# Compressed keys streamed in front of the selected keys, the root's table moved, and the last half block cut in two

## The chip, the cores and the metric

The kernel runs on one core of a Trainium2 chip. The metric is the device time of one execution, in microseconds; lower is better. The kernel before took 977.5 us in the median of three runs (976.83 to 977.7).

The core has a matrix engine (PE, with PEld for its weight loads), a vector engine (DVE), an activation engine (ACT), a general engine (POOL) and a queue engine (SP). Each follows its own fixed list of instructions in order, and semaphores make them wait for one another.

## The reference

One transformer block, in fp32, over 512 tokens of width 1024: a gated feed-forward layer, a mixer with two kinds of attention, a second gated feed-forward layer, and a last normalization.

```python
x = x + 0.5 * swiglu(rmsnorm(x, norm_ffn1), w_gate1, w_up1, w_down1)
x = x + hybrid_mixer(rmsnorm(x, norm_mix), w_in, ..., w_out, rel_bias)
x = x + 0.5 * swiglu(rmsnorm(x, norm_ffn2), w_gate2, w_up2, w_down2)
return rmsnorm(x, norm_final)
```

The mixer has 8 heads of block attention ("MoBA") and 8 heads that add up three attentions over the same query ("NSA"). For an NSA head:

```python
k_cmp = silu(blocks(kc_raw) @ w1_k) @ w2_k               # 31 compressed keys of each group
lg_cmp = q @ k_cmp.T * scale + bias(d_cmp)               # 512 x 31, masked
o_cmp = softmax(lg_cmp) @ v_cmp
o_slc = softmax(q @ ks.T * scale + bias, causal) @ vs    # selected keys: with 512 tokens, all of them
o_win = softmax(q @ kw.T * scale + bias, causal) @ vw    # window keys
out = g0 * o_cmp + g1 * o_slc + g2 * o_win
```

Four heads share one group of keys; there are two groups.

## The kernel before

Every fp32 matrix product is made of products of rounded parts: a value is split into a rounded high part and the remainder (`halves`, ACT line 92 and DVE line 96, or POOL line 94 while `side[0]` is set), and three products (`mm3`, lines 101 to 103) are added in PSUM. For logits, queries and keys are stacked instead: a tile of 128 partitions holds a 64-row part on the one half and its partner on the other (`stack_q`, `stack_k`). `stack_k` copies a half to the other 64 partitions by DMA (line 660).

The program has three stages: the first feed-forward layer, the mixer (it starts near 345 us and ends near 640 us), the second feed-forward layer. PE's list in the mixer is woven from two streams. One is `work`, a stream of projections (`pp`, `pv`, `pc`), the compression of keys and values, and the output projections (`pw`); it runs by the quotas of `target`. The other is `steps`: for each NSA head three chunks with the selected keys (kind "ks"), three with the window keys ("kw"), and after the odd head's "ks" chunks a step for the compressed keys of the pair of heads (`cmp_pair`); then three chunks for each MoBA head. A chunk is one of the groups of query blocks `QIS = ((0, 1), (2,), (3,))`. Each step has three parts: `logits`, `turn` four steps later and `values` seven steps later. The final order of instructions on each engine is set by the framework's own timeline model, so an edit in one place can shift the order in the whole mixer.

A chunk's `logits` takes one of the two PSUM banks of tag "s", multiplies a query block with the keys up to its diagonal (lines 948 and 949, the two stacked key tiles; 128, 256, 384 or 512 columns), then adds the bias and takes the row minimum in one DVE instruction from PSUM (line 954), exponentiates on ACT (956), inverts the sum on DVE (958) and scales on POOL (963). `turn` transposes on PE (972), `values` multiplies with the values (115, 116).

For the compressed keys, `second` (line 805 on) splits the 64 x 64 result `pck` into the tile `kc` with one ACT and one DVE instruction (814, 815) and one DMA (816). `cmp_pair` multiplies, for each of four query blocks and two heads, the query block with 64 columns of `kc` into a bank "s" of its own (line 1011), adds bias and remainder in two DVE instructions of 256 elements (1015, 1016) into the tile `c`, and goes on with a softmax over 32 columns, the transposes (1032) and the values.

The window keys, the selected keys, the token-major values and later the MoBA outputs share twelve tiles `kvn`.

At the end, the last feed-forward product of each of four token blocks `i` comes in two halves of 512 columns (`pd`, six matmuls each). `residual` adds it on DVE (1162) and squares it on ACT with a row sum (1163); after half 1, `norm` takes the root on ACT (1167), inverts it on DVE (1168), scales half 0 on ACT (1170) and half 1 on DVE (1171), and two DMAs on the queue of SP write the block out (1173). The first root needs another ACT table than silu did, which is loaded just ahead of it.

Of the kernel before, what the change touches and what calls it, by code (L numbers as in the profile page):

```python
# [15 lines left out]
S = 512  # L16
# [13 lines left out]
def block_kernel(ctx: ExitStack, tc: tile.TileContext, A: dict, out: bass.AP):  # L30
# [576 lines left out]
    with ExitStack() as ph:  # L607
# [58 lines left out]
        def kvn():  # L666
            return kv.tile([128, S], F32R, name="kvn", tag="kvn", bufs=12)

        def nsa_k(key):
            def then(p):  # L670
                got[key] = stack_k(scaled(p, None), [kvn() for _ in range(4)])
            return then
# [73 lines left out]
        def compress(which):  # L746
# [58 lines left out]
            def second(w):  # L805
                hh, hl = p[2]
                pp = pt(tag, "pck")
                if which == 0:
                    for c in range(2):
                        with held():  # L810
                            mm3(pp[:64, :64], w[c], (hh[:, c], hl[:, c]), c == 0, c == 1)
                    yield
                    a = kv.tile([128, 2, 64], F32R, name="kc")
                    nc.scalar.activation(a[0:64, 0], pp[:64, :64], AF.Copy)
                    nc.vector.tensor_tensor(a[0:64, 1], pp[:64, :64], f32(a[0:64, 0]), ALU.subtract)
                    nc.sync.dma_start(f32(a[64:128]), f32(a[0:64]))
                    got["kc"] = a
                    return
# [93 lines left out]
        def halves_turned(width):  # L912
# [3 lines left out]
                    for name in ("th", "tl")]  # L916

        def chunks_of_head(h, kind, first, last):

# [6 lines left out]
            def logits(qis):  # L926
# [10 lines left out]
                else:  # L937
                    lp = ap.tile([128, 384], F32, name="lpn", tag="lpn", bufs=4)
                at_, wide = {}, 0
                for qi in qis:  # L940
                    at_[qi] = slice(wide, wide + (qi + 1) * 128)
                    wide += (qi + 1) * 128
                for qi in qis:
                    n = (qi + 1) * 128
                    w = at_[qi]
                    lps[qi] = lp[:, w]
                    q = aq[:, qi * 128:(qi + 1) * 128]
                    nc.tensor.matmul(s[:, w], q, ak[at][:, :n], start=True, stop=False)
                    latest[0] = nc.tensor.matmul(s[:, w], q, ak[2 + at][:, :n], start=False, stop=True)
                for qi in qis:  # L950
                    n = (qi + 1) * 128
                    w = at_[qi]
                    m = ap.tile([128, 4], F32, name="m", tag="m", bufs=8)
                    nc.vector.tensor_tensor_reduce(lp[:, w], s[:, w], tb[:, S - n:], -1.0, 3.0e38,
                                                   ALU.add, ALU.min, m[:, 0:1])
                    nc.scalar.activation(lp[:, w], lp[:, w], AF.Exp, bias=m[:, 0:1], scale=-1.0,
                                         accum_out=m[:, 1:2])
                    nc.vector.reciprocal(m[:, 2:3], m[:, 1:2])
# [40 lines left out]
        def cmp_pair(pair):  # L999
# [4 lines left out]
            def logits():  # L1004
                need("kc")
                s = pt("s", "ps_c")
                sv = s.rearrange("p (i h e n) -> p i h e n", i=NT, h=2, e=2)
                for i in range(NT):
                    for odd in range(2):
                        q = got["n", pair][odd][:, i * 128:(i + 1) * 128]  # L1010
                        nc.tensor.matmul(sv[:, i, odd], q, got["kc"][:, :, g * 32:(g + 1) * 32],
                                         start=True, stop=True)
                c = st["c"] = ap.tile([128, NT, 2, 32], F32, name="c", tag="c", bufs=1)
                m = ap.tile([128, 3, NT, 2], F32, name="mc", tag="mc", bufs=2)
                nc.vector.tensor_tensor(c, sv[:, :, :, 0], cb[:, :, 2 * pair:2 * pair + 2, :], ALU.add)
                nc.vector.tensor_tensor(c, c, sv[:, :, :, 1], ALU.add)
                nc.vector.tensor_reduce(m[:, 0], c, AX.X, ALU.max)
# [105 lines left out]
    with ExitStack() as ph:  # L1123
# [35 lines left out]

        def residual(i, half, p):  # L1160

            nc.vector.scalar_tensor_tensor(z[i, half], p, 0.5, z[i, half], ALU.mult, ALU.add)
            nc.scalar.activation(sq, z[i, half], AF.Square, accum_out=ss[:, half, i:i + 1])  # L1163

        def norm(i):
# [6 lines left out]
            for half in range(2):  # L1172
                nc.sync.dma_start(out[i * 128:(i + 1) * 128, half * S:(half + 1) * S], y[half])

# [5 lines left out]
        for i in range(NT):  # L1180
            b = slice(i * 128, (i + 1) * 128)
            for half in range(2):
                p = pt(None, "pd")
                for k, f in enumerate(last):
                    mm3(p, (hs[f][0][:, b], hs[f][1][:, b]), w[half][k], f == last[0], f == last[-1])
                residual(i, half, p)
                if half == 0:
# [91 lines left out]
```

## Time and profile before

| | us |
|---|---|
| median of three runs | 977.5 |
| the profiled execution | 977.13 |
| its span, first to last instruction | 975.3 |
| mean granted TensorE clock | 0.998 |

The profile is of one execution. A row of the timeline starts with its start in us from the span's start, its length, the engine, the line, the operation, and "output<-inputs"; rows of the same kind that follow one another are merged with a count. Matmuls overlap, so the distance from one start to the next, not the length, is what a matmul takes.

| stretch of the mixer, us | DVE busy | ACT busy | POOL busy |
|---|---|---|---|
| 360 to 390 | 22.4 | 18.0 | 0.2 |
| 540 to 570 | 19.3 | 26.3 | 27.5 |
| 600 to 640 | 32.2 | 25.7 | 9.5 |

There are eleven table loads on ACT in the span, each about 1.28 us.

### The profile page before, as it was taken

What the parts mean: (1) busy time and instruction counts of PE and PEld (TensorE: products, weight loads), DVE (VectorE), ACT (ScalarE), POOL (GpSimd) and SP (SyncE); (2) the same over time, 40 slices, a digit from 0 to 9 for tenths busy, and PEclk for the clock granted to TensorE, in tenths of its full rate; (3) what the DMA queues carried; (4) which work ended last, traced back from release to release, by engine and by line L of the source; (5) the groups of instructions that cost most, each with busy time, mean ns of one, the idle gap of its engine ahead of it and who ended that gap; (6) DMA issues with size and microseconds to landing.
All of it is one profiled execution on the core that took longest, in us unless ns stands there. A gap on an engine that the chain in (4) does not pass through costs nothing.

```text
span 975.3 us, 18446 instructions
## 1 busy us (share of the span) xinstructions
PE 962.4 (99%) x6852; PEld 891.4 (91%) x6852; DVE 761.3 (78%) x1557; ACT 565.0 (58%) x1171; POOL 158.6 (16%) x202
## 2 busy tenths in 40 slices
PE   9999999999999999999999999999999999999996
PEld 7789999999999999889888888888999999999995
DVE  6897997788787488867778677889799778778753
ACT  6464664454554366677776886656466445554435
POOL 0000000000000000056777897100000000000002
PEclk9999999999999999999999999999999999999999
DMA  7255544332411225641312332235354423241102
GB/s 259 89 198 160 210 134 136 95 107 80 124 60 53 59 74 148 193 143 40 92 28 71 88 97 71 65 109 194 88 169 134 131 65 106 90 130 44 55 12 87
DMA packets 51599, 104.62 MB, mean 107 GB/s; under 512 B 10129, under 2 KB 16738, under 8 KB 51508
## 3 DMA queue, kind: packets, MB, share of 16 engines
q1 hardware_dynamic: 51220, 102.91, 33.7%
q8 instruction: 54, 0.88, 0.4%
q10 hardware_dynamic: 288, 0.52, 0.2%
q14 instruction: 37, 0.30, 0.1%
HBM read 97.98 MB, written 5.30 MB: 106 GB/s over the span
## 4 chain that ended last, share of the span: by engine, by line
PE 92%; DVE 4%; DMA 2%; ACT 1%; issue 1%; POOL 0%; SPq 0%; ACTq 0%; DVEq 0%; POOLq 0%
PE pd L110 16%; PE pu L101 7%; PE pu L103 7%; PE pu L102 7%; PE pw L103 5%; PE pw L101 5%; PE pw L102 5%; PE pgu L101 3%; PE pgu L102 3%; PE pgu L103 3%; PE pd L102 3%; PE pd L103 3%; PE pd L101 3%; PE ps_t L972 3%; PE pv L103 2%; PE pv L101 2%
## 5 line engine op out<-in xcount | busy, mean ns | idle before, releaser
L242 ACT ACTIVATE sph<-aw 128x512 fp32r<-128x512 f32 x252 | 157.3, 630 | 190.4 <-issue 58.6
L243 DVE TENSOR_TENSOR spl<-aw,sph 128x512 fp32r<-128x512 f32 x252 | 171.2, 686 | 60.2 <-ACT sph L242 57.0
L92 ACT ACTIVATE whi<-raw 128x512 fp32r<-128x512 f32 (+2 forms) x202 | 122.2, 615 | 111.0 <-PE pd L110 33.5
L110 PE MATMUL pd<-h,whi 128*128 128x256 f32 x896 | 138.1, 276 | 0.0
L96 DVE TENSOR_TENSOR wlo<-raw,whi 128x512 fp32r<-128x512 f32 (+1 forms) x166 | 109.1, 666 | 19.8 <-ACT whi L92 16.1
L101 PE MATMUL pu<-th,sph 128*128 128x256 f32 x432 | 119.6, 277 | 0.3 <-ACT wc L352 0.3
L103 PE MATMUL pu<-th,spl 128*128 128x256 f32 x432 | 119.4, 276 | 0.0
L102 PE MATMUL pu<-tl,sph 128*128 128x256 f32 x432 | 119.4, 276 | 0.0
L110 PEld LDWEIGHTS pd<-h,whi 128*128 128x128 f32 x896 | 118.3, 188 | 0.1
L328 DVE TENSOR_TENSOR aw<-aw 128x512 f32<-128x512 f32 x144 | 98.0, 682 | 0.0
L110 PE MATMUL pd<-h,wlo 128*128 128x256 f32 x448 | 87.2, 276 | 0.0
L540 DVE SCALAR_TENSOR_TENSOR x<-pd,x 128x512 f32<-128x512 f32 x88 | 59.9, 684 | 29.6 <-PE pd L110 22.2
L101 PEld LDWEIGHTS pu<-th,sph 128*128 128x128 f32 x432 | 81.1, 188 | 1.2 <-ACT wc L352 0.5
L102 PEld LDWEIGHTS pu<-tl,sph 128*128 128x128 f32 x432 | 81.1, 188 | 0.6
L103 PEld LDWEIGHTS pu<-th,spl 128*128 128x128 f32 x432 | 81.1, 188 | 0.1
L101 PE MATMUL pw<-xo,sph 128*128 128x256 f32 x288 | 79.6, 277 | 0.6 <-ACT sph L242 0.6
L102 PE MATMUL pw<-xo,sph 128*128 128x256 f32 x288 | 79.5, 277 | 0.0
L103 PE MATMUL pw<-xo,spl 128*128 128x256 f32 x288 | 79.4, 277 | 0.0
L110 PEld LDWEIGHTS pd<-h,wlo 128*128 128x128 f32 x448 | 67.4, 188 | 0.0
L881 POOL MEMSET tb<- 128x256 f32 x16 | 4.9, 308 | 332.1 <-DVE x L540 329.0
L1188 POOL TENSOR_SCALAR mean<-ss 128x1 f32<-128x1 f32 x4 | 1.2, 296 | 350.2 <-ACT sqd L1163 350.2
L101 PEld LDWEIGHTS pw<-xo,sph 128*128 128x128 f32 x288 | 54.1, 188 | 1.9 <-ACT sph L242 0.8
(249 smaller groups left out, 2675.8 us busy)
## 6 DMA issues: line engine op xcount, KB each, us to landing
aw<-in_wg SPq DMA_DIRECT2D x72, 256.0 KB, 3.6
aw<-in_wu SPq DMA_DIRECT2D x72, 256.0 KB, 4.7
raw<-in_wd1a SPq DMA_DIRECT2D x20, 512.0 KB, 4.4
raw<-in_wd2a SPq DMA_DIRECT2D x20, 512.0 KB, 5.0
raw<-in_w_a SPq DMA_DIRECT2D x16, 512.0 KB, 3.6
raw<-in_w SPq DMA_DIRECT2D x8, 512.0 KB, 3.6
raw<-in_w_o SPq DMA_DIRECT2D x8, 512.0 KB, 4.0
raw<-in_wg SPq DMA_DIRECT2D x7, 512.0 KB, 3.6
```

The source lines that it names most:

```text
L92: last_hi[0] = nc.scalar.activation(hi, v, AF.Copy)
L96: nc.vector.tensor_tensor(lo, v, f32(hi), ALU.subtract)
L101: nc.tensor.matmul(p, w[0], v[0], start=first, stop=False, skip_group_check=again)
L102: nc.tensor.matmul(p, w[0], v[1], start=False, stop=False, skip_group_check=again)
L103: return nc.tensor.matmul(p, w[1], v[0], start=False, stop=last, skip_group_check=again)
L110: nc.tensor.matmul(p[:, h], a, b[:, h], start=first and n + i == 0, stop=last and n == 2, skip_group_check=True)
L242: nc.scalar.activation(hi, v, AF.Copy)
L243: self.last_lo = nc.vector.tensor_tensor(lo, v, f32(hi), ALU.subtract)
L328: nc.vector.tensor_tensor(to, x, y, op)
L540: nc.vector.scalar_tensor_tensor(xs[d], p, 0.5, xs[d], ALU.mult, ALU.add)
L881: nc.gpsimd.memset(t[:, :S - 256], 0.0)
L972: latest[0] = nc.tensor.transpose(p[:, wide:wide + 128], lps[qi][:, j * 128:(j + 1) * 128], ident)
```

## The change

**Mixer.** Four tiles `kst` of 64 + 512 columns hold the stacked selected keys of the two groups in columns 64 to 575, and the compressed keys of the group in front of them: the high part in columns 32 to 63, its remainder in columns 0 to 31. The write of the compressed keys is done group by group: two ACT instructions in place of one, four of DVE in place of one, four DMAs in place of one. A "ks" chunk's product for query blocks 0, 1 and 2 starts 32 columns earlier, so that its first 32 columns are the compressed logits; for block 3, whose 512 columns fill a bank, one extra product of 64 columns is put into the free rest of block 2's bank. The compressed logits are read from there into `acc`, a tile that is otherwise only used for the sums of squares, by four small DVE instructions for each head (lines 990, 992, 993 and 994 of the new kernel). The own products, the own bank and the two DVE instructions of `cmp_pair` go; its softmax goes on in `acc`, one half for even pairs and one for odd. "ks" chunks now need the compressed keys to be there. `kvn` has eight tiles in place of twelve.

**End.** A root of one column is issued behind the last silu, so that the root's table is loaded there. The very last half block (block 3, half 1) is computed as two parts of 256 columns, each with its own bank, residual and square; the first part's sum is added to `mean` by one more ACT instruction. The first of the last block's two output DMAs is issued by ACT's queue.

```diff
         def kvn():
-            return kv.tile([128, S], F32R, name="kvn", tag="kvn", bufs=12)
+            return kv.tile([128, S], F32R, name="kvn", tag="kvn", bufs=8)
+        CK = 32
+        keys = slice(2 * CK, 2 * CK + S)
+        kst = [kv.tile([128, 2 * CK + S], F32R, name="kst", tag="kst", bufs=4) for _ in range(4)]
...
-                    a = kv.tile([128, 2, 64], F32R, name="kc")
-                    nc.scalar.activation(a[0:64, 0], pp[:64, :64], AF.Copy)
-                    nc.vector.tensor_tensor(a[0:64, 1], pp[:64, :64], f32(a[0:64, 0]), ALU.subtract)
-                    nc.sync.dma_start(f32(a[64:128]), f32(a[0:64]))
+                    lo, hi = slice(0, CK), slice(CK, 2 * CK)
+                    for g in range(2):
+                        v, h, l = pp[:64, g * CK:(g + 1) * CK], kst[g], kst[2 + g]
+                        nc.scalar.activation(h[0:64, hi], v, AF.Copy)
+                        for to in (l[0:64, hi], h[0:64, lo]):
+                            nc.vector.tensor_tensor(to, v, f32(h[0:64, hi]), ALU.subtract)
+                        nc.sync.dma_start(f32(h[64:128, :2 * CK]), f32(h[0:64, :2 * CK]))
+                        nc.sync.dma_start(f32(l[64:128, hi]), f32(l[0:64, hi]))
...
+                    lead = CK if ks and qi < NT - 1 else 0
...
-                    nc.tensor.matmul(s[:, w], q, ak[at][:, :n], start=True, stop=False)
-                    latest[0] = nc.tensor.matmul(s[:, w], q, ak[2 + at][:, :n], start=False, stop=True)
+                    for part in (at, 2 + at):
+                        k = kst[part][:, 2 * CK - lead:2 * CK + n] if ks else ak[part][:, :n]
+                        latest[0] = nc.tensor.matmul(to, q, k, start=part == at, stop=part != at)
+                if ks and qis[0] == 2:
+                    more = s[:, used:used + 2 * CK]
+                    latest[0] = nc.tensor.matmul(more, aq[:, 3 * 128:], kst[at][:, :2 * CK], start=True, stop=True)
...
+                if ks and qis[-1] < NT - 1:
+                    c = cmp_logits(pair)[:, :, odd]
+                    b = cb[:, :, h - 8]
+                    if qis[0] == 0:
+                        v = s[:, :2 * (CK + 128)].rearrange("p (a b) -> p a b", a=2)[:, :, :CK]
+                        nc.vector.tensor_tensor(c[:, 0:2], v, b[:, 0:2], ALU.add)
+                    else:
+                        nc.vector.tensor_tensor(c[:, 2], s[:, :CK], b[:, 2], ALU.add)
+                        nc.vector.tensor_tensor(c[:, 3], more[:, :CK], b[:, 3], ALU.add)
+                        nc.vector.tensor_tensor(c[:, 3], more[:, CK:], c[:, 3], ALU.add)
...
-                        nc.tensor.matmul(sv[:, i, odd], q, got["kc"][:, :, g * 32:(g + 1) * 32],
-                                         start=True, stop=True)
-                nc.vector.tensor_tensor(c, sv[:, :, :, 0], cb[:, :, 2 * pair:2 * pair + 2, :], ALU.add)
-                nc.vector.tensor_tensor(c, c, sv[:, :, :, 1], ALU.add)
...
+        with tc.issue_after(ffn.silu.ins):
+            nc.scalar.activation(rc[:, 0:1], eps, AF.Sqrt)
...
-                nc.sync.dma_start(out[i * 128:(i + 1) * 128, half * S:(half + 1) * S], y[half])
+                (nc.scalar if i == NT - 1 and half == 0 else nc.sync).dma_start(
+                    out[i * 128:(i + 1) * 128, half * S:(half + 1) * S], y[half])
...
+                parts = [slice(0, S)] if (i, half) != (NT - 1, 1) else [slice(0, HT), slice(HT, S)]
+                for n, cols in enumerate(parts):
...
+                    if more:
+                        nc.scalar.activation(mean[:, i:i + 1], sums, AF.Identity, bias=mean[:, i:i + 1], scale=1.0 / D)
```

Outside the mixer and the last 40 us, the order of every engine is as before. Three places show what moved.

**The first "ks" chunk.** On PE, where the first NSA head's first two chunks stand between the last compression products (`pc`), before:

```order
L778 MATMUL pc<-whi,ak 128x256
L948 MATMUL ps_s<-kvn,aq 128x128
L949 MATMUL ps_s<-kvn,aq 128x128
L948 MATMUL ps_s<-kvn,aq 128x256
L949 MATMUL ps_s<-kvn,aq 128x256
L948 MATMUL ps_s<-kvn,aq 128x384
L949 MATMUL ps_s<-kvn,aq 128x384
L101 MATMUL pp<-xo,whi 128x512
```

The same place after the change:

```order
L782 MATMUL pc<-whi,ak 128x256
L967 MATMUL ps_s<-kst,aq 128x160 x2
L967 MATMUL ps_s<-kst,aq 128x288 x2
L967 MATMUL ps_s<-kst,aq 128x416 x2
L970 MATMUL ps_s<-kst,aq 128x64
L101 MATMUL pp<-xo,whi 128x512
```

The products are 32 columns wider, one of 64 columns has come in, and all of them now need the compressed keys. On DVE just ahead of it, where the compressed keys are written and the queries `aq` of the chunk are made, before:

```order
L96 TENSOR_TENSOR wlo<-raw,whi 128x512
L815 TENSOR_TENSOR kc<-pck,kc 64x64
L726 SCALAR_TENSOR_TENSOR vm<-pv,rc,vm 128x4x64
L96 TENSOR_TENSOR wlo<-raw,whi 128x512
L642 SCALAR_TENSOR_TENSOR t<-pp,R 128x512
L96 TENSOR_TENSOR wlo<-raw,whi 128x512 x2
L649 TENSOR_TENSOR aq<-t,aq 64x512 x2
```

And after:

```order
L96 TENSOR_TENSOR wlo<-raw,whi 128x512
L822 TENSOR_TENSOR kst<-pck,kst 64x32 x2
L730 SCALAR_TENSOR_TENSOR vm<-pv,rc,vm 128x4x64
L96 TENSOR_TENSOR wlo<-raw,whi 128x512
L822 TENSOR_TENSOR kst<-pck,kst 64x32 x2
L642 SCALAR_TENSOR_TENSOR t<-pp,R 128x512
L96 TENSOR_TENSOR wlo<-raw,whi 128x512 x2
L649 TENSOR_TENSOR aq<-t,aq 64x512 x2
```

Four small instructions stand ahead of `aq` where there was one.

**The first compressed logits.** On PE, behind the second head's last "ks" chunk, before:

```order
L948 MATMUL ps_s<-kvn,aq 128x512
L949 MATMUL ps_s<-kvn,aq 128x512
L972 MATMUL ps_t<-ident,lpn 128x128 x2
L972 MATMUL ps_t<-ident,lp 128x128
L1011 MATMUL ps_c<-kc,aq 128x64 x8
L101 MATMUL pv<-whi,xo 128x256
```

And after, where the second head's third chunk stands:

```order
L967 MATMUL ps_s<-kst,aq 128x512 x2
L1003 MATMUL ps_t<-ident,lpn 128x128 x2
L1003 MATMUL ps_t<-ident,lp 128x128
L101 MATMUL pv<-whi,xo 128x256
L102 MATMUL pv<-wlo,xo 128x256
```

The eight products of 64 columns are gone. On DVE the chunks' readings change with it; for the first head, after the change (line 975 is the old line 954, and 979 the old 958):

```order
L975 ISA lpn,m<-ps_s,tb 128x256
L975 ISA m 128x1
L990 TENSOR_TENSOR acc<-ps_s,cb 128x2x32
L975 ISA lpn,m<-ps_s,tb 128x384
L975 ISA m 128x1
L96 TENSOR_TENSOR wlo<-raw,whi 128x512
L992 TENSOR_TENSOR acc<-ps_s,cb 128x32
L993 TENSOR_TENSOR acc<-ps_s,cb 128x32
```

The fourth, line 994, comes further down; in five of the eight heads at least one DVE instruction of 384 or 512 columns stands between these readings of the second chunk's bank.

**The end.** On ACT, from the last silu (line 374) to the first root, before:

```order
L374 ACTIVATE t<-pu 128x256
L92 ACTIVATE whi<-raw 128x512
L274 ACTIVATE h<-t 128x512
L92 ACTIVATE whi<-raw 128x512 x2
L1151 ACTIVATE z<-px 128x512 x8
L1163 ACTIVATE sqd,ss<-z 128x512 x2
L1167 ACT_TABLE_LOAD
L1167 ACTIVATE ss<-ss,mean 128x1
```

And after:

```order
L374 ACTIVATE t<-pu 128x256
L1182 ACT_TABLE_LOAD
L1182 ACTIVATE rc<-eps 128x1
L92 ACTIVATE whi<-raw 128x512
L274 ACTIVATE h<-t 128x512
L92 ACTIVATE whi<-raw 128x512 x2
L1172 ACTIVATE z<-px 128x512 x8
L1188 ACTIVATE sqd,ss<-z 128x512 x2
L1192 ACTIVATE ss<-ss,mean 128x1
```

The table load has moved up, ahead of the splits of the last weights. On DVE, the last rows after the change (1187 is the residual, 1193 the reciprocal, 1196 the scaling of half 1):

```order
L1187 SCALAR_TENSOR_TENSOR z<-pd,z 128x512 x2
L1187 SCALAR_TENSOR_TENSOR z<-pd,z 128x256
L1193 RECIPROCAL ss<-ss 128x1
L1196 SCALAR_TENSOR_TENSOR xo<-z,ss,gf 128x512
L1187 SCALAR_TENSOR_TENSOR z<-pd,z 128x256
L1193 RECIPROCAL ss<-ss 128x1
L1196 SCALAR_TENSOR_TENSOR xo<-z,ss,gf 128x512
```

The first part's residual of the last half block now stands ahead of block 2's reciprocal and scaling; before, the whole last residual stood behind them.

More of the change, by code (lines that the diff above doesn't have):

```diff
@@ L666, in kvn @@
         def kvn():
-            return kv.tile([128, S], F32R, name="kvn", tag="kvn", bufs=12)
+            return kv.tile([128, S], F32R, name="kvn", tag="kvn", bufs=8)
+        CK = 32
+        keys = slice(2 * CK, 2 * CK + S)
+        kst = [kv.tile([128, 2 * CK + S], F32R, name="kst", tag="kst", bufs=4) for _ in range(4)]
         def nsa_k(key):
             def then(p):
-                got[key] = stack_k(scaled(p, None), [kvn() for _ in range(4)])
+                got[key] = stack_k(scaled(p, None), [t[:, keys] for t in kst] if key == "ks" else [kvn() for _ in range(4)])
             return then
@@ L812, in second @@
                     yield
-                    a = kv.tile([128, 2, 64], F32R, name="kc")
-                    nc.scalar.activation(a[0:64, 0], pp[:64, :64], AF.Copy)
-                    nc.vector.tensor_tensor(a[0:64, 1], pp[:64, :64], f32(a[0:64, 0]), ALU.subtract)
-                    nc.sync.dma_start(f32(a[64:128]), f32(a[0:64]))
-                    got["kc"] = a
+                    lo, hi = slice(0, CK), slice(CK, 2 * CK)
[6 more added lines that the diff above has]
+                        nc.sync.dma_start(f32(l[64:128, hi]), f32(l[0:64, hi]))
+                    got["kc"] = True
                     return
@@ L916, in halves_turned, with cmp_logits @@
                     for name in ("th", "tl")]
+        def cmp_logits(pair):
+            w = NT * 2 * CK
+            return acc[:, pair % 2 * w:][:, :w].rearrange("p (i h n) -> p i h n", i=NT, h=2)
         def chunks_of_head(h, kind, first, last):
@@ L1004, in logits @@
             def logits():
[L1005 to L1011, printed above, removed]
-                                         start=True, stop=True)
-                c = st["c"] = ap.tile([128, NT, 2, 32], F32, name="c", tag="c", bufs=1)
+                c = st["c"] = cmp_logits(pair)
                 m = ap.tile([128, 3, NT, 2], F32, name="mc", tag="mc", bufs=2)
-                nc.vector.tensor_tensor(c, sv[:, :, :, 0], cb[:, :, 2 * pair:2 * pair + 2, :], ALU.add)
-                nc.vector.tensor_tensor(c, c, sv[:, :, :, 1], ALU.add)
                 nc.vector.tensor_reduce(m[:, 0], c, AX.X, ALU.max)
@@ L1158, in block_kernel, with residual @@
         z = {}
-        def residual(i, half, p):
-            nc.vector.scalar_tensor_tensor(z[i, half], p, 0.5, z[i, half], ALU.mult, ALU.add)
-            nc.scalar.activation(sq, z[i, half], AF.Square, accum_out=ss[:, half, i:i + 1])
+        with tc.issue_after(ffn.silu.ins):
+            nc.scalar.activation(rc[:, 0:1], eps, AF.Sqrt)
+        def residual(i, half, p, cols, sums):
+            y = z[i, half][:, cols]
+            nc.vector.scalar_tensor_tensor(y, p, 0.5, y, ALU.mult, ALU.add)
+            nc.scalar.activation(sq[:, cols], y, AF.Square, accum_out=sums)
         def norm(i):
@@ L1182, in block_kernel @@
             for half in range(2):
[L1183 to L1186, printed above, removed]
+                parts = [slice(0, S)] if (i, half) != (NT - 1, 1) else [slice(0, HT), slice(HT, S)]
+                for n, cols in enumerate(parts):
+                    p = pt(None, "pd")[:, cols]
+                    for k, f in enumerate(last):
+                        mm3(p, (hs[f][0][:, b], hs[f][1][:, b]), [v[:, cols] for v in w[half][k]],
+                            f == last[0], f == last[-1])
+                    more = n < len(parts) - 1
+                    sums = rc[:, 1:2] if more else ss[:, half, i:i + 1]
+                    residual(i, half, p, cols, sums)
+                    if more:
+                        nc.scalar.activation(mean[:, i:i + 1], sums, AF.Identity, bias=mean[:, i:i + 1], scale=1.0 / D)
                 if half == 0:
```

18 lines of the change are left out of this document (11 added, 7 removed).

## The prediction

> **What bounds the kernel now.** I read the page's busy times and its chain first, then the mixer by stretches, then PE's own waits there, and last the timeline of the end.
>
> ```profile
> PE 962.4 (99%) x6852; PEld 891.4 (91%) x6852; DVE 761.3 (78%) x1557; ACT 565.0 (58%) x1171; POOL 158.6 (16%) x202
> ...
> PE 92%; DVE 4%; DMA 2%; ACT 1%; issue 1%; POOL 0%; SPq 0%; ACTq 0%; DVEq 0%; POOLq 0%
> ```
>
> PE is busy for 99% of the span and holds 92% of the chain: a matmul that goes is time that goes, unless PE then waits. Does it wait in the mixer, where the change is? The columns of the next view are the busy us (and instructions) of PE, PEld, DVE, ACT and POOL; below it are the first, one, and the last of eight rows of PE's waits from 400 to 640 us.
>
> ```profile
> 400.00:420.00 20.00, 19.80 (x111) 16.23 (x110) 19.09 (x52) 17.54 (x40) 4.13 (x6) 1.00 0.58 176
> 420.00:540.00 120.00, 119.24 (x737) 104.79 (x736) 88.73 (x284) 87.36 (x220) 83.52 (x103) 1.00 0.22 65
> ```
>
> ```profile
> PEld ps_s L948 <- DVE m L954: 1.3, 3, 0.6
> ...
> PEld pc L777 <- DVE wlo L96: 0.4, 1, 0.4
> ...
> PEld ps_s L948 <- DVE aq L649: 0.2, 1, 0.2
> ```
>
> All eight together are 3.6 us (the five not shown are of 0.3 or 0.4 each). So PE is the bound of the mixer, but in 400 to 420 DVE is nearly full (19.09 of 20 us), and the longest of PE's waits is for a bank "s" that DVE has not yet read. The end of the program is another stage; it is read below.
>
> **The change part by part: PE in the mixer.** What does a narrow product cost, and what 32 more columns?
>
> ```profile
> 436.29 0.97 PEld L1011 LDWEIGHTS ps_c<-kc,aq 128*128 128x128 f32 x8
> 437.18 0.19 PEld L101 LDWEIGHTS pv<-whi,xo 128*128 128x128 f32 x1
> ```
>
> ```profile
> 963.12 0.39 PE L101 MATMUL pd<-whi,h 128*128 128x512 f32 x1
> ...
> 966.29 0.39 PE L103 MATMUL pd<-whi,h 128*128 128x512 f32 x1
> ```
>
> Eight weight loads for the 64-column products take 437.18 - 436.29 = 0.89 us, 0.111 each; the product itself is hidden under the next load. Fifteen matmuls of 512 columns have fourteen distances in 3.17 us, 0.226 each, or 0.442 ns a column. So 32 columns more cost 0.014 us where a product is longer than its weight load, and nothing where it is not (160 columns, 0.071 us, against 0.111).
>
> Removed: 4 pairs x 8 x 0.111 = 3.56 us. Added: 8 extra products of 64 columns x 0.111 = 0.89. Widened: in each of 8 heads two products of 288 and two of 416, 8 x 4 x 0.014 = 0.45. Sum **-2.2 us**; if the 160-column ones paid for their columns too, -2.0.
>
> **What of it comes back: DVE.** Compressed logits now come in small readings.
>
> ```profile
> L958 DVE RECIPROCAL m<-m 128x1 f32<-128x1 f32 x96 | 14.7, 156 | 9.7 <-ACT lpn L956 4.5 <-ACT lp L956 4.5
> ...
> L1015 DVE TENSOR_TENSOR c<-ps_c,cb 128x256 f32<-128x256 f32 x4 | 1.7, 417 | 0.4 <-PE ps_c L1011 0.4
> ...
> L815 DVE TENSOR_TENSOR kc<-pck,kc 64x64 fp32r<-64x64 f32 x1 | 0.2, 209 | 0.0
> ```
>
> No row shows 32 columns; it lies between one column (156 ns) and 64 (209), and nearer to the latter I take 0.18. Each head adds 0.21 + 3 x 0.18 = 0.75 us, 6.0 for eight; four pairs lose two of 0.42 each, 3.4. DVE works 2.6 us longer in a stretch where it idles 120 - 88.7 = 31 us. That is cover, but not at every spot: PE's 3.6 us of waits already exist beside it. I let 0.5 us reach PE; the bounds are 0 and the whole 2.6.
>
> Before the first "ks" chunk there is less cover. The first two rows are DVE's, then two of SP's, one of PE's and one of ACT's.
>
> ```profile
> 405.95 0.21 DVE L815 TENSOR_TENSOR kc<-pck,kc 64x64 fp32r<-64x64 f32 x1
> 406.08 0.47 DVE L726 SCALAR_TENSOR_TENSOR vm<-pv,rc,vm 128x256 fp32r<-128x256 f32 x1
> ```
>
> ```profile
> 406.19 0.47 SPq L816 DMA_DIRECT2D kc<-kc  x1
> 407.18 0.33 SPq L75 DMA_DIRECT2D raw<-in_w_a  x1
> ```
>
> ```profile
> 409.73 0.33 PE L948 MATMUL ps_s<-kvn,aq 128*128 128x128 f32 x1
> ```
>
> ```profile
> 411.63 0.63 ACT L92 ACTIVATE whi<-raw 128x512 fp32r<-128x512 f32 x1 [0.34 <-DMA raw<-in_w_a]
> ```
>
> The one write of `kc` holds DVE for 0.13 us from start to start; four of 32 columns, 0.11 each, hold it for 0.44. Behind them queue the key splits and the queries for which PE waits now (the rows `pc L777` and `aq L649` above), so **+0.3 us** lands on PE (bounds 0 and 0.8, the latter if ACT's second write is late too). On SP three more DMAs of 0.47 us are issued here; the weight load behind them (407.18) leaves some 1.3 us later. ACT already waits 0.34 us for it at 411.63, and the first exponentials are queued behind that split. What hides it is PE's next stretch, 22 products of 512 columns (22 x 0.226 = 5 us) that need none of them; I cost it at nothing, and at 1.3 if that cover is gone.
>
> Mixer: -2.2 + 0.5 + 0.3 = **-1.4 us**.
>
> **The end.** ACT and DVE rows, in order of time; 968.28 to 970.46 is the last block.
>
> ```profile
> 959.95 0.19 ACT L1163 ACTIVATION_READ_ACCUMULATOR sqd<-z 128x1 f32 x1
> 960.21 1.28 ACT L1167 ACT_TABLE_LOAD   x1
> 961.50 0.30 ACT L1167 ACTIVATE ss<-ss,mean 128x1 f32<-128x1 f32 x1
> 962.03 0.75 DVE L1171 SCALAR_TENSOR_TENSOR xo<-z,ss,gf 128x512 f32<-128x512 f32 x1
> 967.61 0.75 DVE L1171 SCALAR_TENSOR_TENSOR xo<-z,ss,gf 128x512 f32<-128x512 f32 x1
> 968.28 0.68 DVE L1162 SCALAR_TENSOR_TENSOR z<-pd,z 128x512 f32<-128x512 f32 x1
> 969.06 0.63 ACT L1163 ACTIVATE sqd<-z 128x512 f32<-128x512 f32 x1 [0.45 <-DVE z L1162]
> 969.87 0.29 ACT L1167 ACTIVATE ss<-ss,mean 128x1 f32<-128x1 f32 x1
> 970.46 0.72 ACT L1170 ACTIVATE xo<-z,ss 128x512 f32<-128x512 f32 x1 [0.29 <-DVE ss L1168]
> ```
>
> The scalings of half 1 are two blocks apart at 962.03 and 967.61: 2.79 us a block, while PE needs 12 x 0.226 = 2.71. The loop over DVE and ACT is the slower, and it started late by the table load. At its end PE's last product starts at 966.29 and ends by 966.68, but its residual starts at 968.28, 1.60 later. Take 1.28 away and it starts at 967.00, still behind PE. So the load goes from the path in full: **-1.28 us**. It runs beside the last PE work instead:
>
> ```profile
> 941.39 0.38 ACT L374 ACTIVATE t<-pu 128x256 f32<-128x256 f32 x1 [0.38 <-PE pu L103]
> 943.26 0.63 ACT L92 ACTIVATE whi<-raw 128x512 fp32r<-128x512 f32 x1 [1.49 <-PE pd L110]
> ```
>
> ACT idles for 1.49 us behind the last silu, waiting for PE; the load (1.28) and a root of one column (0.3) overrun that by 0.1, thirteen microseconds ahead of the products that need those weights. Cost nothing; without the cover, 1.6.
>
> The Trainium skill, "ScalarE: Activation LUTs", section "What ACT_TABLE_LOAD costs", counts a drain of about 1.38 us with each load, 2.66 in all; by it the term would be -2.66. The trace does not agree: from the end of the accumulator's read (960.14) to the root (961.50) there are 1.36 us, the load and little else.
>
> The cut of the last half block does less than it looks. Its first part is ready when six of the twelve 256-column products are done, 0.68 us ahead of 966.68, at 966.0, and DVE takes it ahead of block 2's reciprocal and scaling, which would otherwise stand at 966.33 (967.61 - 1.28). The part takes 0.42 (256 columns from PSUM, the row at 411.90 below), so the scaling moves to about 966.6, the second part starts at 967.3, not 967.0, and ends as the whole would have. The last square is shorter by 0.2 (0.38 for 256 columns in the silu row above, 0.63 for 512), and one ACT instruction of a single column comes in, 0.3 as the root's. I take **+0.1**; bounds -0.4 (no displacement) and +0.6 (the order holds up both engines).
>
> ```profile
> 971.21 1.08 SPq L1173 DMA_DIRECT2D out<-xo  x2
> ...
> out<-xo SPq DMA_DIRECT2D x8, 256.0 KB, 2.3
> ```
>
> The last two issues take 1.08 us, so the second starts 1.08 - 0.33 = 0.75 after the first (0.33 is an issue of 512 KB at 407.18). With two queues both start at once. But both transfers use the same engines, so not all of 0.75 is won; bounds 0 and -0.75, I take the middle, **-0.4**. The Trainium skill, "DMA: Bandwidth & Descriptors", section "Issuing engines are not separate DMA queues", says that issuing from two engines saves only the issue time; by it the term is -0.33. No run here shows two queues at once at the end.
>
> **Sum.** -1.4 - 1.28 + 0.1 - 0.4 = -3.0 us against the profiled execution's 977.13 (span 975.3): **974.2 us**. The median shown is 977.5, 0.4 above that execution, within the spread of the three runs; 0.2% of it, about what a measurement of this kernel tells from no change, is 2.0 us.
>
> **The rivals.**
> *The mixer gives everything back.* DVE's 2.6 us and the reshuffled order of all engines reach PE in full: -2.2 + 2.6 is about zero, and only the end remains, 977.13 - 1.6 = 975.5. For it: PE waits for DVE's reading of "s" already. Against: 31 us of idle DVE. Chance 0.18.
> *The copy of the compressed keys is late.* The first use moves from 436.3 to 409.7, 3.5 us behind the old copy's issue at 406.19.
>
> ```profile
> DMA to landing us min/median/max: 2.2/5.7/5.8
> ```
>
> Copies of keys (`kvn`) landed between 2.2 and 5.8 us after issue. At 5.8, and with the second copy issued 0.5 later, PE waits some 2.2 to 2.8 us once: 976.4 to 977.0. Chance 0.08.
> *The second chunk's bank is held too long*, the slower side. In five heads a DVE instruction of 0.54 to 0.68 us (384 columns at 502.28, 512 at 968.28) stands between the readings of that bank; with three readings of 0.18 it is free some 1.2 us later, and the first chunk's 0.2 later. Where PE wants the bank within that, it stops.
>
> ```profile
> 411.90 0.42 DVE L954 CUSTOM_DVE_ANT_0 lpn<-ps_s,tb 128x256 f32<-128x256 f32 x1
> ...
> 502.28 0.54 DVE L954 CUSTOM_DVE_ANT_0 lpn<-ps_s,tb 128x384 f32<-128x384 f32 x1
> ```
>
> ```profile
> 412.38 0.50 PE L948 MATMUL ps_s<-kvn,aq 128*128 128x512 f32 x1
> ...
> 506.22 0.28 PE L948 MATMUL ps_s<-kvn,aq 128*128 128x128 f32 x1
> ```
>
> PE takes the same bank again with one chunk between. At 412.32 DVE left it 0.06 us before PE took it; at 502.82 it was 3.4 us before. The second is the common case. If five heads of eight were of the first kind, 5 x 1.4 = 7 us would be lost and the time 981. It turns slower than before from a total of 5 us on. Chance 0.07.
> *All lands, and waits go too.* Four banks fewer are taken; if a third of the 3.6 us goes with them and nothing is given back: 977.13 - 2.2 - 1.2 - 1.3 = 972.4. Chance 0.14.
> *The table's switch held more than its row.* If as much again as the load goes with it, 974.2 - 1.3 = 972.9; that is the page's drain. Chance 0.04.
>
> **How the numbers follow.** The forecast has the remaining 0.49. Low end: the rival of vanishing waits with the full issue time, 972.0. High end: the late copy, 977.0; that leaves out the held bank and a little on each side. Faster by over 2.0 us than 977.5 means below 975.5: nearly all of the forecast, both low rivals and a third of "gives everything back", 0.70; within 0.2%: 0.23; slower: 0.07.
>
> **What would show it.** PE's products in the mixer should fall by 32 and gain 8, with its waits near 4.4 us; waits of `ps_s` on DVE above 6 would show the held bank, a wait of the first `ps_s` on DMA the late copy. At the end there should be no table load behind 950 us, the last residual within 0.7 us of PE's last product, and the last two output DMAs on two queues. The prediction is wrong if the mixer is not shorter, or if the end is shorter by less than 1 or more than 2.3 us.

## The result, and the profile after

| | before | changed |
|---|---|---|
| median, us | 977.46 (six runs) | 972.69 (six runs, 972.08 to 973.38) |
| the profiled execution, us | 977.13 | 972.95 |
| its span, us | 975.3 | 971.2 |

The ratio is 0.9949, with a 95% interval of 0.9939 to 0.9959: faster by 4.0 to 6.0 us. The forecast, 974.2, had the sign and the two terms that carry the gain, PE's products and the table's load; the kernel gained over half as much again as forecast.

The program is cut into stages at instructions that both kernels have: the first compression product `pc`, the first product `pgu` of the second feed-forward layer, and the first product of the last half block. First the three PE rows of the timeline before, then those after (start in us, length).

```profile
379.42 0.28 PE L778 MATMUL pc<-whi,ak 128*128 128x256 f32 x1
622.17 0.39 PE L101 MATMUL pgu<-xo,whi 128*128 128x512 f32 x1
965.16 0.39 PE L101 MATMUL pd<-whi,h 128*128 128x512 f32 x1
```

```profile
379.78 0.28 PE L782 MATMUL pc<-whi,ak 128*128 128x256 f32 x1
619.97 0.39 PE L101 MATMUL pgu<-xo,whi 128*128 128x512 f32 x1
962.92 0.28 PE L101 MATMUL pd<-whi,h 128*128 128x256 f32 x1
```

| stage, us | before | changed | difference |
|---|---|---|---|
| up to `pc` (no edit) | 379.42 | 379.78 | +0.36 |
| **mixer**, `pc` to `pgu` | 242.75 | 240.19 | **-2.56** |
| `pgu` to the last half block (no edit but the early root) | 342.99 | 342.95 | -0.04 |
| **end**, to the span's end | 10.14 | 8.28 | **-1.86** |

So the 4.1 us come from where the edits are (-4.4 there, +0.3 elsewhere), and the mixer gave more than the forecast's 1.4. The page's PE line and two stretches of the mixer (PE, PEld, DVE, ACT, POOL):

```profile
PE 960.5 (99%) x6834; PEld 890.0 (92%) x6834; DVE 762.3 (78%) x1585; ACT 567.2 (58%) x1176; POOL 158.5 (16%) x202
...
400.00:420.00 20.00, 19.38 (x109) 15.98 (x109) 18.96 (x51) 16.61 (x37) 2.82 (x4) 1.00 0.53 164
420.00:540.00 120.00, 119.50 (x733) 105.29 (x732) 90.23 (x316) 90.44 (x228) 86.88 (x109) 1.00 0.24 71
```

6834 products are the 6852 of before, less 32, plus 8 for the compressed keys and 6 for the cut. DVE is hardly busier: 1.0 us in the whole program, where the forecast had 2.6 in the mixer alone. The next view has the waits of PE's weight loads from 345 to 645 us (total, times, longest):

```profile
PEld pp L103 <- DVE wlo L96: 0.7, 1, 0.7
PEld ps_t L1003 <- issue: 0.7, 1, 0.7
PEld ps_t L1003 <- POOL lpn L984: 0.5, 2, 0.3
PEld pc L781 <- DVE wlo L96: 0.4, 1, 0.4
PEld ps_s L967 <- PE pc L782: 0.3, 1, 0.3
PEld ps_s L967 <- DVE aq L649: 0.2, 1, 0.2
PEld pct L799 <- ACT hid L790: 0.2, 1, 0.2
```

They are 3.0 us, against 3.6 before and 4.4 forecast. The 1.3 us for a bank "s" behind DVE's minimum is gone, others have come, and no row waits for the copy of the compressed keys.

The end, on ACT, DVE and their queues, in order of time:

```profile
939.54 1.28 ACT L1182 ACT_TABLE_LOAD   x1
940.83 0.20 ACT L1182 ACTIVATE rc<-eps 128x1 f32<-128x1 f32 x1
...
964.36 0.75 DVE L1196 SCALAR_TENSOR_TENSOR xo<-z,ss,gf 128x512 f32<-128x512 f32 x1
965.03 0.42 DVE L1187 SCALAR_TENSOR_TENSOR z<-pd,z 128x256 f32<-128x256 f32 x1
965.08 0.40 ACT L1188 ACTIVATE sqd<-z 128x256 f32<-128x256 f32 x1
965.48 0.41 ACT L1188 ACTIVATE sqd<-z 128x256 f32<-128x256 f32 x1
965.80 0.19 ACT L1188 ACTIVATION_READ_ACCUMULATOR sqd<-z 128x1 f32 x1
965.89 0.28 ACT L1219 ACTIVATE mean<-rc,mean 128x1 f32<-128x1 f32 x1
966.21 0.29 ACT L1192 ACTIVATE ss<-ss,mean 128x1 f32<-128x1 f32 x1
966.79 0.72 ACT L1195 ACTIVATE xo<-z,ss 128x512 f32<-128x512 f32 x1 [0.29 <-DVE ss L1193]
967.51 0.33 SPq L1198 DMA_DIRECT2D out<-xo  x1
967.54 0.37 ACTq L1198 DMA_DIRECT2D out<-xo  x1
```

The table is loaded behind the last silu. The last residual starts 2.11 us behind the half block's first product (before: 968.28 - 965.16 = 3.12), though PE's last product starts at 964.23: it stands behind block 2's scaling. From it to the root are 1.18 us (before 1.59), from the root to the last scaling on ACT 0.58 (0.59), from there to the span's end 4.41 (4.84). These four distances are what the experiments at the end are read by.

### The profile page after: what moved, and what is told of

Read it like the earlier page. It is cut to its first block, busy times and chain, and to the rows that moved or that the text cites. A ratio compares the mean times of both kernels' runs of the same rounds, so it can differ in the third digit from the quotient of the medians.

```text
span 971.2 us, 18438 instructions
## 1 busy us (share of the span) xinstructions
PE 960.5 (99%) x6834; PEld 890.0 (92%) x6834; DVE 762.3 (78%) x1585; ACT 567.2 (58%) x1176; POOL 158.5 (16%) x202
## 4 chain that ended last, share of the span: by engine, by line
PE 56%; DVE 1%; ACT 1%; issue 0%; POOL 0%; ACTq 0%; POOLq 0%
PE pd L110 8%; PE pu L101 3%; PE pu L102 3%; PE pu L103 3%; PE pw L101 3%; PE pw L102 3%; PE pw L103 3%; PE ps_s L967 3%; PE ps_t L1003 3%; PE pp L103 2%; PE pp L101 2%; PE pp L102 2%; PE po L116 2%; PE pgu L101 2%; PE pgu L102 1%; PE pgu L103 1%
```

## The experiments

One execution's time says little about half a microsecond, so each edit is read from the distances in its own stage. Time and ratio of every run (the ratio to the kernel before on the same chip, with its 95% interval), the mixer, and the four distances of the end:

| run | median, us | ratio | mixer | to residual | to root | to scaling | to span's end |
|---|---|---|---|---|---|---|---|
| before | 977.46 | | 242.75 | 3.12 | 1.59 | 0.59 | 4.84 |
| changed | 972.69 | 0.9949 (0.9939 to 0.9959) | 240.19 | 2.11 | 1.18 | 0.58 | 4.41 |
| e1_end_only | 975.58 | 0.9982 (0.9973 to 0.9990) | 242.47 | 2.11 | 1.18 | 0.59 | 4.73 |
| e2_mixer_only | 974.73 | 0.9968 (0.9956 to 0.9981) | 239.83 | 3.12 | 1.59 | 0.59 | 4.47 |
| e3_no_cut | 973.06 | 0.9959 (0.9945 to 0.9973) | 241.27 | 1.85 | 1.59 | 0.58 | 4.39 |
| e4_late_root | 973.10 | 0.9959 (0.9946 to 0.9971) | 239.98 | 3.12 | 1.34 | 0.59 | 4.34 |
| e5_one_queue | 972.89 | 0.9955 (0.9941 to 0.9968) | 240.13 | 2.11 | 1.18 | 0.59 | 4.42 |
| e6_thrice | 973.24 | 0.9961 (0.9949 to 0.9974) | 240.00 | 2.11 | 1.18 | 0.59 | 4.60 |
| e7_mean_on_dve | 972.57 | 0.9956 (0.9944 to 0.9969) | 240.31 | 2.11 | 1.59 | 0.58 | 4.33 |
| e8_copies_halved | 973.15 | 0.9959 (0.9946 to 0.9971) | 240.12 | 2.11 | 1.18 | 0.59 | 4.48 |
| e9_weights_on_dve | 973.53 | 0.9954 (0.9942 to 0.9967) | 239.98 | 2.11 | 1.18 | 0.52 | 4.44 |
| e10_four_products | 975.41 | 0.9975 (0.9966 to 0.9984) | 242.43 | 2.11 | 1.18 | 0.58 | 4.34 |
| e11_ninefold | 979.09 | 1.0013 (1.0004 to 1.0022) | 246.78 | 2.11 | 1.18 | 0.59 | 4.39 |
| e12_addition_first | 973.58 | 0.9961 (0.9948 to 0.9975) | 239.63 | 2.11 | 0.99 | 0.52 | 4.57 |

**Do the two halves add up?** The kernel before with only one half of the diff each: e1_end_only has the edits from `sq = tmp.tile` on, e2_mixer_only all those ahead of it.

> The kernel before with the three edits of the end alone (early root, last half block in two, second queue for the last but one output). Read from PE's first product of the last half block to the span's end: 10.14 us before, 8.28 in the changed kernel. Theory, the parts are independent: the mixer keeps its 242.75 us from the first pc product to the first pgu product behind it, the end takes 8.3 +- 0.2, the time is 977.5 - 1.9 = 975.6. Rival, the end depends on how the mixer went: then the end is not 8.3 but nearer to 9 or to 7.5.

> The kernel before with the edit of the mixer alone. Theory: the products' sum of -2.2 us comes through whole and DVE gives nothing back, since its narrow readings take 0.10 us each from start to start and not the 0.18 of their rows: the mixer takes 240.2 +- 0.3 us instead of 242.75, the end keeps 10.1, the time is 977.5 - 2.6 = 974.9. Rival, the forecast's 0.8 us of give-back exist and the changed kernel's trace hid them by chance: mixer 241.3, time 976.1.

-1.80 and -2.65 us by the medians, -4.45 together, against -4.77 for both (-4.0 to -6.0): the halves add up within what the runs can tell. e2's mixer is 239.83: the products' gain comes through whole. The rival's 241.3 turns up once, in e3_no_cut, whose mixer is the same; the other seven kernels with this mixer lie between 239.6 and 240.3, against 242.47 and 242.75 with the old one. So that rival does not fit, and one trace of a mixer can be off by a microsecond. e1's end is 8.61, longer than the expected 8.3, and all of the excess is in the last distance, 4.73; the three ahead of it repeat the changed kernel's to 0.01 us. What follows the last scaling differs from run to run.

**The parts of the end.**

```diff
# e3_no_cut
-parts = [slice(0, S)] if (i, half) != (NT - 1, 1) else [slice(0, HT), slice(HT, S)]
+parts = [slice(0, S)]
# e4_late_root
-with tc.issue_after(ffn.silu.ins):
-    nc.scalar.activation(rc[:, 0:1], eps, AF.Sqrt)
# e5_one_queue
-(nc.scalar if i == NT - 1 and half == 0 else nc.sync).dma_start(
+nc.sync.dma_start(
```

> The changed kernel with its last half block whole again. Theory, from the rows of both traces: the load that left is worth 1.28 and the queue 0.43, so the cut is worth what is left of 1.86, 0.15: the end takes 8.4 us instead of 8.28. Rival A, the cut is worth the whole 0.41 by which the path from the last residual to the root got shorter: 8.7. Rival B, the cut costs 0.1 as forecast: 8.2.

> The changed kernel without the root behind the last silu, so that the table is loaded at the first root of the norm again. Theory: the load's row of 1.28 us comes back in full: the end takes 9.5 us instead of 8.28. Rival A, a drain beside the load comes back too: 10.9. Rival B, the loop of DVE and ACT makes part of it good before the end, because the last half block comes in two: 9.0 or less.

> The changed kernel with its last two output DMAs both issued by SP. The end behind the last scaling on ACT (from its start to the span's end) was 4.84 and 4.47 us in two kernels with one queue, 4.34, 4.39, 4.41 and 4.73 in four with two. Theory, the queue is worth about 0.25 on average and less than the forecast's 0.4: 4.5 to 4.8 here, time 972.9 to 973.1. Rival A, the queue is worth the whole distance of two issues, 0.75: above 5.0. Rival B, it is worth nothing since both transfers use the same engines: 4.4.

The residual and the root in e3_no_cut, DVE and ACT (the half block's first product is at 962.89):

```profile
964.74 0.68 DVE L1187 SCALAR_TENSOR_TENSOR z<-pd,z 128x512 f32<-128x512 f32 x1
966.33 0.29 ACT L1192 ACTIVATE ss<-ss,mean 128x1 f32<-128x1 f32 x1
```

Without the cut the residual starts 1.85 us behind the first product, not 3.12: 1.27 us less, where the row of the table's load is 1.28. No drain beside it comes to light. The cut then costs 0.26 (2.11, as the first part pushes block 2's scaling, and with it the second part, back) and wins 0.41 up to the root: 0.15 in all, theory's number and neither rival's. In e4_late_root the first two distances are 4.46 against 3.29, 1.17 more and not the full 1.28: where the loop is late the cut displaces nothing (3.12, as before) and wins 0.25 of the root's way. Theory's 9.5 for the end is nearest (9.39), and neither rival fits. Its median is only 0.4 us above the changed kernel's, which alone would have misled.

In e5_one_queue both issues stand on SP, 0.43 us apart; the second row is the latter of the two, and the third the last issue of the kernel before:

```profile
967.83 0.81 SPq L1198 DMA_DIRECT2D out<-xo  x2
968.26 0.37 SPq L1198 DMA_DIRECT2D out<-xo  x1
971.95 0.33 SPq L1173 DMA_DIRECT2D out<-xo  x1
```

The last distance is 4.42. One queue gave 4.84, 4.47 and 4.42, two queues 4.33 to 4.73 in eleven kernels (mean 4.46). My 0.25 is not borne out: the second queue is worth nothing that these runs can see. The issues show where its gain goes. In the changed kernel the last issue starts 0.75 us behind the last scaling on ACT, in e5 1.18; but from that issue to the span's end are 3.66 us in the changed kernel (3.6 to 4.0 in the eleven with two queues) and 3.24 in e5 (3.2 to 3.4 in the three with one). What the issue gains, the transfers lose; that they slow each other down when they start together is likely and not shown. Of the 0.43 between the first two traces, 0.31 is that the two issues of the kernel before stood 0.74 apart (971.21 and 971.95) and not 0.43 as in e5 or 0.44 as in e2.

**Does DVE's time reach PE?** The three additions that stand first are repeated: `for _ in range(3)` in e6_thrice, `range(9)` in e11_ninefold.

> The changed kernel with the additions of the 64-column reading and of the first two 32-column readings done three times over in each head (the same values are written again), so that DVE has 2 x 8 x (0.137 + 0.10 + 0.10) = 5.4 us more by the distances from start to start, up to 9.3 by the rows' durations (0.22 + 0.18 + 0.18). Theory, DVE's time in the mixer is covered: the mixer (first pc product to first pgu product behind it) takes 239.8 to 241.3 as in the four kernels with the new mixer, PE's waits for ps_s stay under 1 us in all. Rival A, DVE's work reaches PE whole: 245 or more. Rival B, a fifth reaches it, as the forecast had it (0.5 of 2.6): 241.3 to 242.2.

> As e6_thrice, with the three additions done nine times over, so that DVE has four times that kernel's surplus: it had 5.1 us more in 380 to 640 us than the changed kernel, so some 20 us here, of the 55 that DVE idles in 420 to 640. Theory, the cover of DVE in the mixer is wide and its work does not reach PE before the idle time at a place is used up: the mixer 240 to 242.5. Rival, the cover is local and thin: the banks of s are held 1.5 to 2.7 us longer per chunk and PE stops for them, ps_s waits of several us, mixer 245 to 255.

The stretch from 380 to 640 us in the changed kernel, in e6 and in e11 (PE, PEld, DVE, ACT, POOL):

```profile
380.00:640.00 260.00, 258.88 (x1495) 224.59 (x1494) 197.69 (x579) 192.51 (x448) 150.33 (x184) 1.00 0.33 96
380.00:640.00 260.00, 258.81 (x1498) 224.94 (x1497) 202.75 (x628) 193.01 (x448) 150.83 (x184) 1.00 0.32 96
380.00:640.00 260.00, 254.39 (x1460) 219.15 (x1459) 215.46 (x767) 190.25 (x443) 150.07 (x184) 1.00 0.31 92
```

e6's 5 us more of DVE left no mark beyond the scatter: 240.00, where a fifth of them would have given 241.2. e11 shows where the cover ends. Its stretch of 420 to 540 us, then the largest waits of its weight loads and those for the bank "s", and last the largest row of PE's own waits:

```profile
420.00:540.00 120.00, 116.36 (x704) 100.81 (x705) 105.94 (x481) 86.04 (x215) 82.15 (x101) 1.00 0.21 67
```

```profile
PEld ps_t L1005 <- issue: 3.1, 3, 1.8
PEld pp L103 <- DVE wlo L96: 1.3, 1, 1.3
...
PEld ps_s L967 <- DVE m L975: 0.5, 1, 0.5
PEld ps_s L967 <- DVE acc L991: 0.5, 1, 0.5
...
PE ps_t L1005 <- DVE acc L991: 1.5, 1, 1.5
```

From 380 to 640 us DVE had 215.5 us against 197.7, 17.8 more; the window ends earlier in e11's longer program, and over the whole program DVE had 783.0 against 762.3, 20.7 more. The mixer lost 6.6, a third of that, and the listed waits of the weight loads from 345 to 645 us grew as much, from 3.0 to 9.7. Theory's 240 to 242.5 is missed; the rival's 245 to 255 holds, though not by its mechanism, for the waits behind the bank are 1.0 us and the larger ones, 5.3 in all, stand at the transposes `ps_t`. The last row names the repeated additions (line 991 here) as what released one of these; the path from them to the transposes was not followed further. Somewhere between 5 and 20 us of surplus DVE's work begins to reach PE, although DVE still idles 14 of the 120 us from 420 to 540: the cover is gone at places, not in all.

**What is a narrow product worth?** e10_four_products repeats `more`'s product, `for _ in range(4)`.

> The changed kernel with the 64-column product of each second chunk done four times (the same values are written again): 8 x 3 = 24 products more. Theory, each takes the 0.111 us of a weight load, as in the forecast's sum: the mixer 240.1 + 2.7 = 242.8 +- 0.5, time 972.7 + 2.7 = 975.4. Rival, a product that waits in a bank beside DVE's readings costs more: 244 or more. Rival, repeated products with the same weights cost only their columns, 64 x 0.442 ns = 0.028 each: 240.8.

242.43 is 2.24 above the changed kernel's mixer, and as much above 240.17, the mean of the eight kernels with an unaltered new mixer (239.63 to 241.27): 0.09 for each of 24 products; by the medians 2.72, 0.113 each. A weight load's time and not the columns' 0.028 is what such a product costs, as the sum of -2.2 had it.

**How close was the copy?** Each copy goes in two DMAs of 32 partitions.

> The changed kernel with each of its four copies of compressed keys issued as two DMAs of 32 partitions: 8 issues of about 0.5 us instead of 4, the last copy some 2 us later, and the weight load behind them too. The copies of the first group were issued at 406.31 and 406.88 and landed within 1.9 to 2.4 us, by 408.8 to 409.3, and the first product that reads them starts at 410.14. Theory, a copy up to 1 us later is still in time, and the later weight load is covered: the mixer takes 239.8 to 241.3, no wait for a kst DMA above 0.3 us. Rival, the copies are already at the edge: PE waits 0.5 to 2 us for the DMA at its first ps_s product, mixer 241 to 242.5.

The mixer is 240.12, and PE's gap ahead of the first `ps_s` grows by 0.16 us (0.20 to 0.36). By the order of SP the first group's last copy is the fourth issue of eight; it stands at 408.82, 28.2 us behind `pc`, where the second of four stood at 406.88, 27.1 behind it. It landed 2.0 us after its issue, at 410.8, and the weight load of the first `ps_s` starts at 410.85: 0.87 us behind the start of `aq` on DVE, where it was 0.74 in the changed kernel. The waits' view puts it down to `aq` all the same. So the slack was about 1 us and is now used up. The weight load behind the copies, 29.0 us behind `pc` in the changed kernel, stands 31.4 behind it here and cost nothing.

**A version that beats both?** The one-column addition, 0.28 us on ACT between the last square and the root, goes to DVE, which idles there. e9 and e12 move the product with the norm's weights off POOL as well; e12 holds it behind the addition.

```diff
# e7_mean_on_dve
-nc.scalar.activation(mean[:, i:i + 1], sums, AF.Identity, bias=mean[:, i:i + 1], scale=1.0 / D)
+nc.vector.scalar_tensor_tensor(mean[:, i:i + 1], sums, 1.0 / D, mean[:, i:i + 1], ALU.mult, ALU.add)
# e9_weights_on_dve, besides: for the last block, ahead of norm(i)
-nc.gpsimd.tensor_tensor(z[i, 0], z[i, 0], gf[0], ALU.mult)
+nc.vector.tensor_tensor(z[i, 0], z[i, 0], gf[0], ALU.mult)
# e12_addition_first: the product inside
+with tc.issue_after(added.ins):
```

> The changed kernel with the one-column addition of the first part's sum done by DVE, which is idle there, instead of by ACT between the last square and the root. Theory: the 0.28 us row of ACT and its gap leave the path: from the last residual to the root 0.86 us instead of 1.18, the end 8.0 instead of 8.29, time 972.4. Rival, the addition stands in DVE's queue ahead of the last residual or of the reciprocal and its result comes late: the distance stays at 1.18 or grows.

> The changed kernel with both the one-column addition and the last block's product of half 0 with the norm's weights moved to DVE, the product behind the addition; POOL has nothing but the one-column mean of half 0 left in the last block. In e7_mean_on_dve the addition's row was 0.84 us and ended 0.02 us from the end of POOL's 1.26 us product beside it. Theory, DVE's instruction with two inputs in SBUF was held until POOL's product had ended: without POOL's product the addition takes 0.2 us, the last residual to the root 0.85 to 0.95 us (1.18 in the changed kernel, 1.59 in e7), the root to the last scaling on ACT 0.6 to 0.8, the end 0.2 us shorter than the changed kernel's, too little for the timed runs. Rival, the addition waits for ACT's accumulator whatever POOL does: the addition again 0.5 us or more, 1.4 or more to the root.

> As e9_weights_on_dve, with the product with the norm's weights held behind the one-column addition on DVE (there it stood ahead of it, and the addition began 0.94 us behind the last residual). Theory: the addition begins some 0.55 us behind the last residual, as soon as ACT's accumulator is read, and takes 0.2; the last residual to the root 0.85 to 0.95 us (1.18 in the changed kernel), the root to the last scaling on ACT 0.6 to 0.75, since the reciprocal now waits for the product; the two together 1.55 +- 0.1 instead of 1.77. The time is 0.2 us below the changed kernel's, which the timed runs cannot tell: 972 to 973.5. Rival, the product holds up the reciprocal by its whole 0.68: the two together 1.8 or more.

e7 made the way to the root longer, 1.59, because a sum of one column took 0.84 us. POOL's product and DVE's addition in e7, then DVE's in e12:

```profile
964.31 1.26 POOL L1222 TENSOR_TENSOR z<-z,gf 128x512 f32<-128x512 f32 x1
964.75 0.84 DVE L1219 SCALAR_TENSOR_TENSOR mean<-rc,mean 128x1 f32<-128x1 f32 x1 [0.23 <-ACT sqd L1188]
```

```profile
966.37 0.16 DVE L1219 SCALAR_TENSOR_TENSOR mean<-rc,mean 128x1 f32<-128x1 f32 x1 [0.23 <-ACT sqd L1188]
```

964.75 + 0.84 = 965.59, and POOL's product ends at 965.57. Without it the same addition takes 0.15 (e9) and 0.16 (e12): it was held. e9's distance stayed at 1.18 since the scheduler put the product ahead of the addition. In e12, root and scaling come 0.99 + 0.52 = 1.51 us behind the residual instead of 1.76: 0.25 us won on the path, as expected, and nothing in the time (973.58, 972.66 to 975.17). No version measurably faster than the changed kernel was found.

## Why the prediction was right, and where it was short

- **PE's products, -2.2: right.** The counts came as forecast; with 0.111 us for a weight load and 0.443 ns a column, 24 products fewer and 32 wide ones that grew by 32 columns make -2.2, and e10 bears out the price.
- **DVE's surplus, +2.6 of which +0.5 on PE: the step that failed.** The forecast put 0.18 us for each narrow reading "between one column (156 ns) and 64 (209)", the length of a row. The rows after, for one head:

```profile
436.51 0.19 DVE L992 TENSOR_TENSOR acc<-ps_s,cb 128x32 f32<-128x32 f32 x1
436.61 0.18 DVE L993 TENSOR_TENSOR acc<-ps_s,cb 128x32 f32<-128x32 f32 x1
436.83 0.19 DVE L994 TENSOR_TENSOR acc<-ps_s,acc 128x32 f32<-128x32 f32 x1
437.05 0.75 DVE L649 TENSOR_TENSOR aq<-t,aq 64x512 fp32r<-64x512 f32 x1
```

  The length was right and the price was not: the next instruction starts 0.10 us later, 0.22 where it needs the result (993 to 994), and in some places, as ahead of `aq` here, 0.22 though it does not. The eight heads' readings hold DVE for 4.0 us by the distances, not 6.0; the eight that went, 0.42 long, held it for 3.0, not 3.4. The key writes had been costed by the distance (0.11), the readings by the length: the two terms did not use one measure. And in e6 even twice the forecast's surplus reached PE with nothing that stands out of the scatter.
- **The early DVE work, +0.3: nothing seen.** PE's gap at the first `ps_s` product is 0.20 us before and after, the wait for `wlo` at `pc` 0.35 before and 0.41 after.
- **The mixer, -1.4 in all: -2.56 in the trace, -2.65 in e2.** The rest beyond the products, 0.3, may be waits that went (the listed ones fell from 3.6 to 3.0 us), but it lies within what the mixer varies from run to run. So the first half of the rival "all lands, and waits go too", which had 0.14, came true: nothing was given back. Of the 1.2 us of waits that it added, 0.6 at most is seen, that they went because four banks fewer are taken was not tested, and its 972.4 leaves out the cut and the queue: that it is near the measured time is in part luck.
- **The table's load, -1.28: right**, 1.27 in e3's distance. The Trainium skill's 2.66, a drain included ("ScalarE: Activation LUTs", "What ACT_TABLE_LOAD costs"), is not borne out here: neither e3 nor e4 shows more than the row. So the rival of the switch that held more than its row, 972.9, is near the measured time by chance.
- **The cut, +0.1: -0.15.** Its displacement came as forecast (0.26 against 0.3), and so did the shorter residual and square. What was mis-sized is the added ACT instruction. Before, ACT stood idle ahead of the root, in the row here and the root's at 969.87:

```profile
969.59 0.19 ACT L1163 ACTIVATION_READ_ACCUMULATOR sqd<-z 128x1 f32 x1
```

  From this reading to the root are 0.28 us, though the reading is 0.19 long and other instructions follow such a reading after 0.09. The added instruction does not need the last sum and stands in that wait: from the reading to the root are 0.41 now (965.80 to 966.21), 0.13 more and not 0.3.
- **The second queue, -0.4: right by chance, and a term that failed.** The first two traces differ by 0.43, e5 shows no loss without it. The forecast took half of 0.75 between two issues; the issues are 0.43 apart in e5, and what the second queue saves there comes back behind the last issue (3.66 us against 3.24).
- **The copy, SP's delay, the held bank: as forecast**, no wait in the rows; e8 puts the copy's slack at about a microsecond, so that rival was nearer than its 0.08 said.

The forecast started from an execution of 977.13, 0.33 below the median of the six runs; against that median its sum of -3.0 would be 974.5. Of the 1.8 us down to 972.69 the mixer's terms are 1.2 and the cut 0.25, while the queue's 0.4, which the runs do not bear out, counts the other way. So the terms that the experiments bear out, 2.56, 1.27 and 0.15, make 4.0, the lower end of the measured 4.0 to 6.0; the 0.8 up to the median's 4.8 has no cause that is shown.

## What to carry to other kernels

Cost an instruction by the distance to the next start on its engine, in every term, and by the row's length, or a little more, only where a successor needs the result. To price work on an engine off the bound, double it and triple it: a dose shows whether the cover holds (5 us: nothing) and where it ends (some 20 us: a third of it lost). Judge an edit of half a microsecond by the distances between named instructions, not by a time that scatters by more.

## What the runs showed of the hardware

- **POOL and DVE hold one another up.** DVE's one-column addition with both inputs in SBUF took 0.84 us beside POOL's product and ended with it, 0.15 and 0.16 without. The other way round, POOL's one-column mean in the changed kernel:

```profile
956.54 0.19 POOL L1221 TENSOR_SCALAR mean<-ss 128x1 f32<-128x1 f32 x1 [345.91 <-ACT sqd L1188]
964.65 0.51 POOL L1221 TENSOR_SCALAR mean<-ss 128x1 f32<-128x1 f32 x1 [1.15 <-ACT sqd L1188]
```

  The second ran beside DVE's scaling (964.36 to 965.11), whose inputs are in SBUF, and ended at 965.16; the first beside a residual with an input in PSUM. The Trainium skill, "SBUF — State Buffer", section "Who interferes with whom", has it that a DVE instruction with two inputs in SBUF contends with a GpSimd instruction that reads SBUF, and that this contention is an exclusive lock; these rows agree.
- **DVE's rows overlap**: 0.18 us long, 0.10 from start to start.
- **Two output DMAs that start together take longer than two that start 0.43 us apart**: 3.6 to 4.0 us from the last issue to the span's end in eleven kernels, 3.2 to 3.4 in three (one of these, the kernel before, has them 0.74 apart).
- **The same stage differs by microseconds between kernels that leave it alone.** From `pgu` to the last half block it took 341.72 us in e9 and 344.57 in e11, with the same products in all. That scatter, more than the edits' ends, sets what a time can tell.
